# Mamba's half of an output projection moved in front of RWKV's inversion, for both segments at once

## The chip, the cores and the metric

One core of a Trainium2 chip runs the whole program in one launch. The metric is the device time in microseconds (us), the median of several executions.

## The reference

Two layers of a hybrid model over 256 context tokens (segment 0) and 256 latent tokens (segment 1), D = 1024, all in 32-bit floats. Each layer gets six modulation vectors per segment from `silu(c) @ w_ada + b_ada`. Layer 0 has an RWKV-7 mixer (8 heads of 64) and a Mamba-2 mixer (8 heads of 64) side by side; their outputs are concatenated, 512 columns each, and one projection `mix_w_out` (1024 x 1024) brings them back to the stream. A dense SwiGLU (2816 wide) follows. Layer 1 is a windowed attention in which only latent tokens ask, and a mixture of 8 experts. What the change is about:

```python
def finish(h, p, y_rw, y_mb):
    ...
    return jnp.concatenate([o_rw, y_mb], axis=-1).astype(h.dtype) @ w_out
...
h_lat = h_lat + m_lat[2] * o_lat
h_lat = h_lat + m_lat[5] * channel_mixer(_modulate(_rms_norm(h_lat, norm_ffn[i]), m_lat[3], m_lat[4]))
```

The same two lines stand for `h_ctx`. The projection is linear, so it can be made as RWKV's 512 rows of `w_out` plus Mamba's 512 rows.

## The kernel before

Activations lie with features on the 128 partitions and tokens along the free side: `hS[seg]` and `moS[seg]` are [128, 8, 256], block k holding features 128k to 128k+127. In `moS[seg]` blocks 0 to 3 are RWKV's output and 4 to 7 Mamba's.

**Weights.** Every weight is an entry of the list `stream`, in the order in which it is used: a chunk of 128 x 1024 floats, 512 KB (1 MB for the experts). `get_raw` (L82) hands out a chunk and emits loads up to 15 entries ahead, into a ring of four buffers `wraw`, all on SP's queue. So a chunk is loaded when the chunk four places earlier has been used up. `split_ws` (L374) turns a chunk into two halves of 128 x 512, and each into a rounded part `whi` (ScalarE, L393) and a rest `wlo` (L395, VectorE; GpSimd for every third chunk among the first 30 from `mo_first`). `project` (L399) makes three matmuls of 256 columns for each 128 x 128 block of weights and segment: hi x hi, lo weight x hi, hi weight x lo (L418).

**Modulation.** `ada_steps` (L281) multiplies the two vectors by 16 chunks of `w_ada`, eight matmul records a chunk (L290), and after each eighth chunk puts the sums in place by way of ScalarE (L295, L302) and GpSimd (L303). The first 16 chunks are made at the start. The other 80 steps, one chunk each, are a generator `ada_z`, and `tick(seg, n)` (L818) draws n steps of it while segment 0 is in the mixer, each tied behind the last PE instruction (`issue_after`). That is a lower bound only: a planner with a timeline of its own orders every engine's instructions when the program is built, so a step can stand later than its tick.

**The mixer of segment 0.** `mixer(0)` (L1113) handles both halves of RWKV's heads at once. `prepare` for each of four head pairs (11 ticks each) builds scaled operands, `operands` (2 ticks each) transposes them; then 8 ticks, then `invert` (L935): 31 steps of two VectorE instructions (L949, L951), each needing the one before, on tiles of 128 partitions. `merge` and the four steps of `chain` for each half (2 ticks in the first three) need the inverted blocks; then `finish` (L1075) in five rounds, one tick each, writes `moS`. All ticks that are left are drained, the context rows are loaded and transposed into `hS[0]` by `load_h` (16 transposes L1176, 4 copies L1177).

**After it.** `mixer(1)` (two halves one after the other, each with its own inversion) and `mix_ffn(0)` (L1208) are independent, and the planner interleaves them. `mix_ffn` projects `moS` in four column blocks of two chunks each (8 blocks of k), adds the gated result to `hS` (L1205), takes the norm's sums (squares on ScalarE, 16 matmuls with a column of ones, L352, for segment 0) and runs the SwiGLU. Then `load_h(1)` fetches x by GpSimd's queue into a tile of the next pool, and `mix_ffn(1)` follows. In layer 1's norm GpSimd adds up the four squares (L349).

## Time and profile before

| what | us |
|---|---|
| three timed runs | 1999.26, 2011.8, 2014.42 |
| median | 2011.8 |
| the profiled execution | 1999.02 |
| its span | 1997.1 |

The profile is of one execution, the one of 1999.02 us. Its stages, from the span's start: 0 to 230 the first modulation, input projection and Mamba; 237 to 302 RWKV's operands for segment 0; 302 to 340 the inversion; 340 to 385 merge and chain; 385 to 403 finish; 403 to 735 the SwiGLU of segment 0 among the mixer of segment 1; 757 to 778 the output projection of segment 1; then its SwiGLU, layer 1 and from about 1200 us on the experts. "x" is a count of records; PEclk is the share of the full TensorE clock that was granted (0.50 is 1.2 GHz, 1.00 is 2.4 GHz).

### The profile page before, as it was taken

What the parts mean: (1) busy time and instruction counts of PE and PEld (TensorE: products, weight loads), DVE (VectorE), ACT (ScalarE), POOL (GpSimd) and SP (SyncE); (2) the same over time, 40 slices, a digit from 0 to 9 for tenths busy, and PEclk for the clock granted to TensorE, in tenths of its full rate; (3) what the DMA queues carried; (4) which work ended last, traced back from release to release, by engine and by line L of the source; (5) the groups of instructions that cost most, each with busy time, mean ns of one, the idle gap of its engine ahead of it and who ended that gap; (6) DMA issues with size and microseconds to landing.
All of it is one profiled execution on the core that took longest, in us unless ns stands there. A gap on an engine that the chain in (4) does not pass through costs nothing.

```text
span 1997.1 us, 35257 instructions
## 1 busy us (share of the span) xinstructions
PE 1906.8 (95%) x13590; PEld 1610.6 (81%) x13590; DVE 1589.5 (80%) x2519; ACT 1225.1 (61%) x1912; POOL 204.1 (10%) x236
## 2 busy tenths in 40 slices
PE   6999997988999989999999979999999999999997
PEld 3886663777989989999999777888888888888885
DVE  5877677489599667666689768898999999999997
ACT  4555432345454455555578738777778787777775
POOL 4033230041120010000011220000000000000000
PEclk8999896988999999999999989999999999999998
DMA  7342388542335464555654548999999999999991
GB/s 277 104 111 85 115 284 292 175 142 87 118 101 175 128 177 145 170 182 181 199 165 131 201 158 319 355 347 347 354 362 362 332 363 354 361 334 356 347 351 53
DMA packets 266705, 459.34 MB, mean 230 GB/s; under 512 B 13325, under 2 KB 145585, under 8 KB 266529
## 3 DMA queue, kind: packets, MB, share of 16 engines
q1 hardware_dynamic: 257616, 438.80, 64.8%
q0 software_dynamic: 4496, 13.79, 2.3%
q10 hardware_dynamic: 4416, 4.41, 0.8%
q8 instruction: 109, 1.79, 0.4%
q14 instruction: 68, 0.55, 0.1%
HBM read 455.88 MB, written 1.08 MB: 229 GB/s over the span
## 4 chain that ended last, share of the span: by engine, by line
PE 85%; DVE 6%; DMA 5%; issue 2%; ACT 1%; POOL 1%; ACTq 0%; DVEq 0%; POOLq 0%
PE a L418 26%; PE b L1669 8%; PE b L1670 8%; PE b L1668 8%; PE ch L1719 4%; PE ch L1720 4%; PE ch L1718 4%; PE b L813 3%; DMA wraw<-in_w_ada_dram 3%; PE ch L813 2%; PE a L290 2%; PE y L418 2%; PE b L418 2%; DVE wlo L395 1%; PE y L813 1%
## 5 line engine op out<-in xcount | busy, mean ns | idle before, releaser
L395 DVE TENSOR_TENSOR wlo<-wraw,whi 128x1024 fp32r<-128x1024 f32 (+2 forms) x974 | 929.7, 975 | 203.2 <-ACT whi L393 193.7
L393 ACT ACTIVATE whi<-wraw 128x1024 fp32r<-128x1024 f32 (+2 forms) x996 | 830.9, 844 | 399.6 <-PE a L418 192.2
L1669 PE MATMUL b<-wlo,eH 128*128 128x512 f32 (+1 forms) x768 | 288.9, 376 | 2.0 <-DVE wlo L395 1.6
L1670 PE MATMUL b<-whi,eL 128*128 128x512 f32 (+1 forms) x768 | 285.5, 372 | 0.0
L418 PE MATMUL a<-xH,whi 128*128 128x256 f32 x928 | 267.8, 289 | 7.0 <-DVE su L1232 5.9
L1668 PE MATMUL b<-whi,eH 128*128 128x512 f32 (+1 forms) x768 | 272.7, 374 | 0.0
L418 PE MATMUL a<-xL,whi 128*128 128x256 f32 x928 | 267.3, 288 | 1.8 <-DVE xL L365 1.8
L418 PE MATMUL a<-xH,wlo 128*128 128x256 f32 x928 | 267.1, 289 | 0.9 <-DVE wlo L395 0.9
L418 PEld LDWEIGHTS a<-xH,whi 128*128 128x128 f32 x928 | 180.7, 195 | 10.7 <-DVE su L1232 6.2
L418 PEld LDWEIGHTS a<-xL,whi 128*128 128x128 f32 x928 | 180.5, 195 | 5.2 <-DVE xL L365 2.5
L418 PEld LDWEIGHTS a<-xH,wlo 128*128 128x128 f32 x928 | 180.0, 194 | 4.1 <-issue 1.6
L1669 PEld LDWEIGHTS b<-wlo,eH 128*128 128x128 f32 x768 | 144.8, 189 | 29.4 <-DVE wlo L395 5.0
L1668 PEld LDWEIGHTS b<-whi,eH 128*128 128x128 f32 x768 | 144.3, 188 | 26.7 <-ACT whi L393 1.5
L1670 PEld LDWEIGHTS b<-whi,eL 128*128 128x128 f32 x768 | 144.7, 188 | 24.8
L1719 PE MATMUL ch<-wlo,gH 128*128 128x512 f32 x352 | 140.2, 398 | 0.3 <-DVE wlo L395 0.3
L1720 PE MATMUL ch<-whi,gL 128*128 128x512 f32 x352 | 138.9, 395 | 0.0
L1718 PE MATMUL ch<-whi,gH 128*128 128x512 f32 x352 | 115.7, 395 | 0.0
L418 PE MATMUL a<-gL,whi 128*128 128x256 f32 x352 | 99.1, 284 | 1.0 <-DVE gL L372 1.0
L418 PE MATMUL a<-gH,whi 128*128 128x256 f32 x352 | 99.5, 286 | 0.0
L418 PE MATMUL a<-gH,wlo 128*128 128x256 f32 x352 | 98.8, 285 | 0.0
L290 PE MATMUL a<-wraw,cpad 128*32 128x256 f32 x768 | 71.5, 465 | 17.7 <-DMA wraw<-in_w_ada_dram 16.4
L1719 PEld LDWEIGHTS ch<-wlo,gH 128*128 128x128 f32 x352 | 66.1, 188 | 16.2 <-DVE wlo L395 1.0
(614 smaller groups left out, 3381.9 us busy)
## 6 DMA issues: line engine op xcount, KB each, us to landing
wraw<-in_moe_w_dram SPq DMA_DIRECT2D x254, 1024.0 KB, 6.2
wraw<-in_w_ada_dram SPq DMA_DIRECT2D x96, 512.0 KB, 5.3
wraw<-in_ffn_w_dram SPq DMA_DIRECT2D x88, 512.0 KB, 4.0
wraw<-in_na_w_qkv_dram SPq DMA_DIRECT2D x40, 512.0 KB, 3.7
wraw<-in_ffn_w_dram SPq DMA_DIRECT2D x48, 384.0 KB, 3.1
wraw<-in_mix_w_in_dram SPq DMA_DIRECT2D x24, 512.0 KB, 3.7
wraw<-in_mix_w_out_dram SPq DMA_DIRECT2D x16, 512.0 KB, 5.1
wraw<-in_moe_w_dram POOLq DMA_DIRECT2D x7, 1024.0 KB, 11.4
```

Of the source, the lines that this page charges most:

```text
L290: T.matmul(p[32 * j:32 * j + 32, 0:256], cpad[:, ko, :], w[:, 256 * j:256 * j + 256], start=ko == 0, stop=ko == KO - 1, skip_group_check=True)
L393: S.activation(hi, x, AF.Copy)
L395: (G if on_pool else eng or V).tensor_tensor(lo, x, hi.bitcast(F32), OP.subtract)
L418: T.matmul(bs[bi][0:m1 - m0, o:o + n], w_[:, k, m0:m1], x[part][:, kx, x[2]], start=bi not in begun, stop=last, skip_group_check=True)
L813: pe[0] = T.matmul(*args, **kw)
L1668: T.matmul(ps[k][:, 0:w], eH[:, ko, :], wh[:, i, :], start=ko == 0, stop=False)
L1669: T.matmul(ps[k][:, 0:w], eH[:, ko, :], wl[:, i, :], start=False, stop=False)
L1670: T.matmul(ps[k][:, 0:w], eL[:, ko, :], wh[:, i, :], start=False, stop=ko == KO - 1)
L1718: T.matmul(ps[n], gH[:, kf, :], wh[:, w, c_], start=kf == 0, stop=False)
L1719: T.matmul(ps[n], gH[:, kf, :], wl[:, w, c_], start=False, stop=False)
L1720: T.matmul(ps[n], gL[:, kf, :], wh[:, w, c_], start=False, stop=kf == 21)
```

## The change

- Mamba's output goes into a tile `moM` [128, 4, 512] for both segments, RWKV's into `moR`. `mamba_out` multiplies `moM` by Mamba's 512 rows of `mix_w_out`: it splits `moM` on ScalarE and GpSimd, then for each of four chunks (`split_ws(ci, G)`: rests on GpSimd) makes 24 matmuls of 512 columns, and ScalarE puts the sums, scaled by the gate, into a DRAM tensor `mom` by way of SP's queue, 256 KB at a time. It is called in three parts: after the operands of the third and fourth head pair, and in front of `invert`.
- `load_h` reads `mom` back (1 MB a segment), and VectorE adds the transposed rows to it. Segment 0's is called after the first round of `finish`; there the first chunk of RWKV's half is split too. Segment 1's stands in `mix_ffn(0)` behind the projection; x comes by the ring.
- The projections in `mix_ffn` have one chunk per column block in place of two.
- Modulation: 6 steps ahead of `mixer(0)`; 8 ticks in `prepare`, 2 in `operands` of the first two pairs, none in front of `invert`; 3, 3, 3, 1 in the chain's steps; 3 in each round of `finish`. In the stream Mamba's four chunks stand behind step 42, the context and RWKV's first chunk behind step 62.
- The norm's squares are taken column block by column block in `mix_ffn`; the first three are added on GpSimd, so 8 matmuls with ones are left.
- `zg` moves to another pool, so that segment 0's RWKV operands can be given up earlier.

```diff
@@ get_raw's stream
+    def between(n):
+        if n == 42:
+            for c0 in range(0, D, 256):
+                mom_ch.append(chunk(w_cols(a["mix_w_out"], 512 * D, D, range(4), c0, 256), (4, 256)))
+        if n == 62:
+            x_ch.extend(chunk(dram(a["ctx"], 128 * t * D, [[D, 128], [1, D]]), (D,)) for t in range(2))
+            mo_ch.append([mo_block(0)])
...
-        mo_ch.append([col_chunks(a["mix_w_out"], 0, D, c0, 256, KS) for c0 in range(0, D, 256)])
+        mo_ch[seg] += [mo_block(c0) for c0 in range(0 if seg else 256, D, 256)]
+        if seg == 0:
+            xl_ch = [chunk(dram(a["x"], 128 * t * D, [[D, 128], [1, D]]), (D,)) for t in range(2)]
...
+    def mamba_out():
+        moL = []
+        xh = []
+        for i in range(2):
+            xh.append(mt([128, 2, NT], "xmh", "BG", 2, F32R))
+            xl = []
+            for j in range(2):
+                S.activation(xh[i][:, j, :], moM[:, 2 * i + j, :], AF.Copy)
+                xl.append(wsp.tile([128, NT], F32R, name="moml", tag=("whi", "wlo")[j], bufs=nsplit[0]))
+                G.tensor_tensor(xl[j], moM[:, 2 * i + j, :], xh[i][:, j, :].bitcast(F32), OP.subtract)
+            moL += xl
+            if i == 0:
+                yield
+        xl = res.tile([128, 4, NT], F32R, name="moL", tag="h8")
+        for k in range(4):
+            S.activation(xl[:, k, :], moL[k].bitcast(F32), AF.Copy)
+        yield
+        for b, ci in enumerate(mom_ch):
+            ps = [bank("a b") for m in range(2)]
+            for ks, wh, wl in split_ws(ci, G):
+                for m in range(2):
+                    for k in range(ks.start, ks.stop):
+                        h, i = xh[k // 2][:, k % 2, :], k - ks.start
+                        w = slice(128 * m, 128 * m + 128)
+                        mm(ps[m], wh[:, i, w], h, start=k == 0, stop=False, skip_group_check=True)
+                        mm(ps[m], wl[:, i, w], h, start=False, stop=False, skip_group_check=True)
+                        mm(ps[m], wh[:, i, w], xl[:, k, :], start=False, stop=k == 3, skip_group_check=True)
+            for m in range(2):
+                ft = 2 * b + m
+                o = wsp.tile([128, NT], F32, name="momo", tag=("whi", "wlo")[m], bufs=nsplit[0])
+                for seg in range(2):
+                    t = slice(256 * seg, 256 * seg + 256)
+                    S.activation(o[:, t], ps[m][:, t], AF.Copy, scale=mods[0][:, 16 + ft, MOD[seg]:MOD[seg] + 1])
+                SY.dma_start(mom[128 * ft:128 * ft + 128, :], o)
...
+    def load_h(seg, chs, tag):
+        xt = [get_raw(i) for i in chs]
+        hS[seg] = (hcp, res)[seg].tile([128, KO, 256], F32, name="h", tag=("hc", "h8")[seg])
+        SY.dma_start(hS[seg], mom.rearrange("(k p) t -> p k t", p=128)[:, :, 256 * seg:256 * seg + 256])
+        for k in range(0, KO, 2):
...
+            V.tensor_tensor(h, p, h, OP.add)
...
@@ mixer
             if len(group) > 1:
-                tick(seg, 8)
+                next(m_)
                 X0s = unpack_both(AAs, invert(AAs))
...
+                if seg == 0 and hcp is None:
+                    context_next()
+                tick(seg, 3)
+    for _ in range(6):
+        next(ada_z)
     mixer(0)
@@ mix_ffn
-        for k in range(0, KO, 4):
-            split(x[0][:, k:k + 4, :], x[1][:, k:k + 4, :], moS[seg][:, k:k + 4, :], "s")
+        split(x[0][:, 0:4, :], x[1][:, 0:4, :], moS[seg], "s")
...
+            norm_sums(hS[seg], fp, 2 * i, acc, G)
+        if seg == 0:
+            load_h(1, xl_ch, "a")
```

## Rows read from the trace of the kernel before

**Rows 1.** The page's chain of waits that ended last, shares by engine.
```profile
PE 85%; DVE 6%; DMA 5%; issue 2%; ACT 1%; POOL 1%; ACTq 0%; DVEq 0%; POOLq 0%
```

**Rows 2.** Busy time by stage, core 0: stretch, its length, engines, PEclk, DMA share, GB/s.
```profile
237.20:302.10 64.90, 62.97 (x586) 38.73 (x582) 46.81 (x100) 19.33 (x50) 18.94 (x24) 0.93 0.86 282
302.10:340.00 37.90, 26.54 (x260) 9.90 (x256) 31.00 (x68) 9.13 (x20) 2.58 (x5) 0.70 0.92 309
340.00:385.30 45.30, 43.63 (x1056) 34.58 (x1048) 17.65 (x44) 14.01 (x38) 0.85 (x4) 0.83 0.57 188
385.30:402.50 17.20, 16.86 (x115) 8.07 (x113) 9.40 (x20) 7.37 (x12) 1.74 (x3) 0.90 0.56 167
402.50:412.70 10.20, 6.65 (x39) 5.18 (x39) 7.33 (x11) 6.75 (x15) 3.97 (x4) 0.69 0.60 201
412.70:455.00 42.30, 39.58 (x324) 35.17 (x324) 37.71 (x79) 19.14 (x38) 17.67 (x16) 0.95 0.40 121
455.00:500.00 45.00, 37.01 (x311) 33.59 (x310) 42.45 (x94) 23.54 (x44) 8.14 (x6) 0.85 0.28 83
500.00:735.00 235.00, 231.08 (x2484) 215.39 (x2484) 173.36 (x362) 114.69 (x218) 22.10 (x21) 0.99 0.44 133
735.00:757.00 22.00, 16.83 (x104) 15.74 (x102) 8.95 (x19) 8.25 (x14) 4.23 (x4) 0.77 0.78 180
757.00:778.00 21.00, 21.00 (x175) 20.76 (x174) 20.14 (x44) 13.61 (x25) 3.59 (x5) 1.00 0.48 151
```

**Rows 3.** Waits that ended in 235 to 345: us in total, times, longest.
```profile
PEld a L290 <- DMA wraw<-in_w_ada_dram: 25.2, 20, 3.4
PE a L290 <- DMA wraw<-in_w_ada_dram: 12.0, 16, 3.0
```

**Rows 4.** Line L290 (modulation) by stage: PE and PEld busy, records; eight are a chunk.
```profile
237.20:302.10 64.90, 24.11 (x292) 6.79 (x288) 0.93 0.86 282
302.10:340.00 37.90, 19.78 (x180) 4.19 (x176) 0.70 0.92 309
340.00:385.30 45.30, 9.04 (x112) 2.88 (x104) 0.83 0.57 188
385.30:403.40 18.10, 5.97 (x64) 1.85 (x64) 0.91 0.58 178
```

**Rows 5.** VectorE's groups in 302.1 to 340: busy, mean ns, idle time before.
```profile
L951 DVE TENSOR_TENSOR Xu<-Xu,tm 128x31 f32<-128x31 f32 (+15 forms) x31 | 10.6, 343 | 1.0
L949 DVE TENSOR_TENSOR tm<-Au,Xu 128x31 f32<-128x31 f32 (+15 forms) x31 | 10.6, 343 | 1.1
L313 DVE SCALAR_TENSOR_TENSOR g<-mod,PV 128x16 f32<-128x16 f32 x1 | 0.2, 176 | 4.7 <-POOL mod L303 4.7
```

**Rows 6.** Timeline of segment 1's first inversion beside GpSimd: start, us, engine, instruction.
```profile
457.23 0.38 DVE L951 TENSOR_TENSOR Xu<-Xu,tm 64x220 f32<-64x220 f32 x1
457.23 1.54 POOL L395 TENSOR_TENSOR wlo<-wraw,whi 128x512 fp32r<-128x512 f32 x1 [5.01 <-ACT whi L393]
457.64 1.38 DVE L949 TENSOR_TENSOR tm<-Au,Xu 64x231 f32<-64x231 f32 x1
```

**Rows 7.** The chain that ended last, in order of time: start, us, engine, line, records.
```profile
51.55 1.36 PE y L418 x6
...
458.75 4.50 PE a L352 x32
...
595.93 48.09 PE a L418 x399
```

**Rows 8.** GpSimd's rests of weights in 225 to 420: duration ns min/median/max, first and last start.
```profile
L395 POOL TENSOR_TENSOR wlo<-wraw,whi x2: 1266/1336/1405, 406.7 to 408.0; 128x512 fp32r<-128x512 f32 x2
```

**Rows 9.** VectorE in 385 to 413, an addition of 128 x 512.
```profile
L1106 DVE TENSOR_TENSOR yrw<-yrw,moc 128x512 f32<-128x512 f32 x2 | 1.4, 692 | 0.1
```

**Rows 10.** Waits that ended in 730 to 805.
```profile
ACT sq L348 <- issue: 4.5, 1, 4.5
PE a L1176 <- DVE h L1205: 4.0, 1, 4.0
```

More of the change, by code (lines that the diff above doesn't have):

```diff
@@ L39, in hybrid_kernel @@
     cscr = dp.tile([16, NT], F32, name="cscr")
+    mom = dp.tile([D, NT], F32, name="mom")
     def dram_row(t, n):
@@ L158, in hybrid_kernel @@
     hS = [None, None]
-    moS = [res.tile([128, KO, 256], F32, name="moc", tag="h8"), res.tile([128, KO, 256], F32, name="mol")]
+    moM = res.tile([128, 4, NT], F32, name="moM", tag="h8")
+    moR = res.tile([128, 2, 4, 256], F32, name="moR", tag="mol")
+    moS = [moR[:, seg] for seg in range(2)]
     c0 = pool(c0s, "c0")
@@ L393, in split_ws @@
                 S.activation(hi, x, AF.Copy)
-            on_pool = 0 <= i - mo_first and (lambda n, k: n<30 and n%3==0)(i - mo_first, k0 // step)
+            on_pool = 0 <= i - mo_first and i < mo_first + 30 and (i - mo_first) % 3 == 0
             (G if on_pool else eng or V).tensor_tensor(lo, x, hi.bitcast(F32), OP.subtract)
@@ L397, in split_ws @@
         return out_
+    ready = {}
     def project(chs, xs, use, w=256, tag="a"):
@@ L410, in project @@
         for k0, ci in chs:
-            for ks, wh, wl in split_ws(ci):
+            for ks, wh, wl in ready.pop(ci, None) or split_ws(ci):
                 for i, (m0, m1) in enumerate(ms):
@@ L559, in hybrid_kernel @@
     S.dma_start(gup, a["rw_g_up"][0])
+    zg = [mkp.tile([96, 256], F32, name=f"zg{seg}") for seg in range(2)]
     mbs = ctx.enter_context(ExitStack())
@@ L706, in hybrid_kernel @@
             for seg in range(2):
-                y = moS[seg][:, 4 + hp, :]
+                y = moM[:, hp, 256 * seg:256 * seg + 256]
                 tk = slice(256 * seg, 256 * seg + 256)
@@ L715, in hybrid_kernel @@
             sq = bt([128, NT], "sqm", "cb", bufs=2)
-            for seg in range(2):
-                S.activation(sq[:, 256 * seg:256 * seg + 256], moS[seg][:, 4 + 2 * g_ + h, :], AF.Square)
+            S.activation(sq, moM[:, 2 * g_ + h, :], AF.Square)
             for j in range(4):
@@ L726, in hybrid_kernel @@
             for seg in range(2):
-                y = moS[seg][:, 4 + hp, :]
+                y = moM[:, hp, 256 * seg:256 * seg + 256]
                 V.scalar_tensor_tensor(y, y, pv("mnw", hp), p[:, 256 * seg:256 * seg + 256], OP.mult, OP.mult)
@@ L1295, in values_of @@
         return last
-    load_h(1, [xt[:, t] for t in range(2)])
     for r2 in range(2):
```

99 lines of the change are left out of this document (58 added, 41 removed).

## The prediction

> **What bounds the kernel now.** I read the chain of waits first: PE holds 85% of it [rows 1], so work taken off PE counts where PE has no gaps. Busy time by stage says where that is [rows 2]: in 500 to 735 PE is busy 231.08 of 235 us, in 757 to 778 all 21.00, both at full clock. Other stages end otherwise. In 237 to 302 PE is busy 62.97 of 64.9 us, but 24.11 us of that are modulation matmuls, 36.5 chunks [rows 4]. In 302 to 340 the DMA rings run at 309 GB/s, PE waits for modulation chunks (25.2 and 12.0 us from 235 to 345 [rows 3]) and nobody minds, because VectorE's inversion ends this stage; that chain is held 4.7 us by one instruction that waits for a modulation sum [rows 5]. In 340 to 403 merge, chain and finish step between PE, ScalarE and VectorE, with the DMA rings half idle (0.57 and 0.56). In 402.5 to 412.7 PE is busy 6.65 us at a clock of 0.69: finish is over, the context's transposes and the first weights are not there. From 412.7 to 500 VectorE is busy 37.71 of 42.3 and 42.45 of 45 us, PE 39.58 and 37.01. In 735 to 757 PE has 16.83 of 22 us at a clock of 0.77 [rows 2].
>
> The idea of the change follows from this: PE is idle or on work nobody waits for while VectorE inverts, and the projection can lie there. I go through it stage by stage against the profiled execution, 1999.0 us (span 1997.1 and 1.9 around it).
>
> **Operands, 237 to 302.** Six modulation chunks are used up before the mixer, and each head pair draws 8 ticks in place of 11. A chunk costs PE 24.11/36.5 = 0.66 us here [rows 4]. Six of them are 4 us, but they now stand in Mamba's stage, where PE is busy too; I take half, and 3 us for waits on chunks that come later: -5 us. Ends: 0, if the planner puts the same number of steps before the inversion as now (36 of the 42 still fit), and -10, if all six and all waits go.
>
> **The inversion, 302 to 340.** The 4.7 us go: by the count of records (36.5 chunks up to 302 and 22.5 in the inversion [rows 4]) the sum that L313 waits for, half-way in, comes of chunk 48 of 80, and after the change only 42 are drawn by then. Against it stands GpSimd. Twelve of its instructions of 128 x 512 are new here (four rests of `moM`, eight of weights), 1.27 to 1.41 us each [rows 8], and none runs during the inversion today. What one does to an inversion is to be seen at 457: the step beside it takes 1.38 us, its neighbour of nearly the same size 0.38 [rows 6], so 1.0 us is lost; at least ten of the twelve fall into the inversion: +10 us. Together +5; ends: -5 (all twelve before it) and +12 (12 x 1.0, and the stall only moved).
> The Trainium skill, SBUF — State Buffer, section Who interferes with whom, states that a VectorE instruction with two SBUF inputs and a GpSimd instruction that reads SBUF exclude one another for a whole instruction. The two rows agree in kind; by the rule up to 1.34 us could be lost each time, 13 us in place of 10, and the time below would be 1981.
>
> Does PE finish under it? Mamba's half is 4 chunks x 24 = 96 matmuls of 512 columns. Six take 1.36 us [rows 7], 0.227 each: 21.8 us, twice that at 1.2 GHz. PE's own work in this stage is 26.54 - 19.78 = 6.8 us [rows 2, 4], so they are ready some 10 to 14 us into the inversion, whose VectorE part is then 38 - 4.7 + 10 = 43 us long: end after 36, or 58 at the low level throughout. I take 0, ends 0 and +15. The put to DRAM (8 x 256 KB) finds the rings free, since no modulation is drawn until the chain: 0, at most +5 for the 4 MB written and read back at about 309 GB/s with part of them exposed; the reading of `mom` stands 40 us behind the put. No row shows a store of this kind, hence the bound.
>
> **Merge, chain, finish, 340 to 403.** Here the steps come back: 20 ticks in the chain for 12, 15 in finish for 5, 18 more on a path where PE is one of the links. A chunk costs 9.04/14 = 0.65 us [rows 4], 11.7 us in all; where PE waits for a copy it is hidden. I take half, +6; ends 0 and +12. The rings: 4 of Mamba's chunks, 38 of modulation, the context's 2 and RWKV's first come behind step 42. A chunk of 0.524 MB at 309 GB/s takes 1.70 us; the chain needs 16 new ones in 45 us and is not starved.
>
> **From finish to the first projection, 402.5 to 412.7.** The context's transposes and the first weights stand ready now, and half of `moS` is to be split. But behind the chain the ring still has 17 chunks of modulation and 3 of RWKV's half to load, 20 x 1.70 = 34 us, against 27.4 from the chain's end to the first matmul today. So only the first block starts early: -3; ends -9 and +5. The additions on VectorE, 0.69 each [rows 9], replace copies on ScalarE.
>
> **The projection of segment 0, 412.7 to 500.** 96 of 192 matmuls of 256 columns go, 48.09/399 = 0.1205 us each: 11.6 us. Half of the 32 records with ones go: 2.25 of 4.50 us [rows 7]. PE is within 3 us of full up to 455 and short in the gap after it, where an earlier SwiGLU fills what the inversion leaves. Sum -14; ends: -5, if VectorE is the bound there (it loses splits of weights, but gains four additions of 0.69 us), and -16.
>
> **735 to 778.** Segment 1's 16 transposes leave the transition; PE waits 4.0 us with them behind VectorE, and ScalarE stands 4.5 us behind an issue [rows 10]: the first goes, the second needn't. -5 of the 22 us; ends 0 and -9. Then another 96 matmuls, here with no gap at all: 96 x 0.1205 = -11.6; ends -9 and -12. Layer 1's norms trade one addition on GpSimd for four matmuls: 0, +-2.
>
> **Sum.** -5 + 5 + 6 - 3 - 14 - 5 - 11.6 = -27.6, so 1971.4 for an execution like the profiled one. That one equals the fastest of the three timed runs; their median, 2011.8, is 12.8 us higher. Nothing in the profile says which of the two a new median will be like, so I add half of it: 1978.
>
> **The rivals.**
> *The gaps fill up* (for it: the 8 us without PE in 455 to 500 and the 10 us of 402.5 to 412.7; against it: VectorE is 94% busy there). The 18 ticks are hidden (-6), the start gains its full 9 (-6), and the SwiGLU runs under the inversion (-12): 1978 - 24 = 1954.
> *The first projection isn't shortened*: it is late by its weights (34 us of loads behind the chain) and by VectorE, not by PE. For it: VectorE's 37.71 of 42.3 us and a ring of four. Then the -14 goes and the -3 becomes +5: 1978 + 22 = 2000, no change that can be told.
> *Mamba's half doesn't lie under the inversion but ahead of merge* (the slower side). Its rests and weight splits go through GpSimd, which VectorE holds up in turn; if the matmuls get going only when the inversion ends, and at 1.2 GHz as PE does in this stage now (clock 0.70, then 0.83 [rows 2]), 96 x 0.454 = 43.6 us stand on the path: 1978 + 43.6 = 2021.6, slower than before. It decides from 27.6 us on, that is from about three fifths of the matmuls exposed at that level. Against it: PE comes into the inversion from a stage with a clock of 0.93, and the twelve GpSimd instructions are only 16 us.
>
> **How the numbers follow.** Forecast 0.50, gaps filled 0.20, no shorter projection 0.20, ahead of merge 0.10. The worst ends added up reach +43 us and the best -63, but not together. 8 in 10: from 1948, just below the first rival, to 2010, half-way into the last one. About 1% (20 us) is what a measurement can tell from no change: faster means under 1992. The forecast gives 0.45 of that (14 us of margin) and 0.05 same; the first rival 0.20 faster; the second 0.01 faster, 0.18 same, 0.01 slower; the last 0.05 same and 0.05 slower. Together 0.66, 0.28, 0.06.
>
> **What would show it.** Right: the inversion free of the 4.7 us idle time but with about ten steps of 1.3 us beside GpSimd; 96 matmuls of 512 columns that end before merge; modulation records up in 340 to 403 from 22 to about 38 chunks; both projections at 96 matmuls of 256 columns; the stretch of 21 us at 757 cut by more than 9. Wrong: merge's first matmul more than 45 us after the inversion's first transpose; PE waiting for chunks in the chain; a projection of segment 0 that ends no earlier after the chain than now; or an output projection of segment 1 that isn't shorter because its weights are late.

## The result, and the profile after

The changed kernel takes 2028.9 us (median of 20 runs, 2007.5 to 2039.4), the kernel before 2005.9 beside it (20 runs, 1994.3 to 2017.7): the ratio is 1.009, 95% interval 1.0066 to 1.0115. It is slower by 0.9% (the medians lie 23.0 us apart), where 1978 was forecast; that lies outside the range too. The time of an execution goes with its mean granted clock: the four shortest of the changed kernel, 2007.5 to 2018.3 us, have 0.962 to 0.966, the five longest, 2034.7 to 2039.4, have 0.952 to 0.954, and nine of ten executions of the kernel before (those timed beside the experiments) lie between 0.960 and 0.967. The profiled execution took 2034.9 us, 2033.1 from first to last instruction, against 1997.1 before: 36.0 us more, since it is one of the long ones and the one of the kernel before a short one.

I cut both executions at the same instructions. *Operands* runs from 237.2 to the inversion's first VectorE step, *inversion* from there to the start of its last full transpose (tile `XT`), *merge and chain* to ScalarE's copy of the first Y, *finish* to the first matmul of segment 0's projection, *projection and SwiGLU 0* to the last matmul of its down projection, *to SwiGLU 1* to the first down-projection matmul of segment 1; the rest is layer 1.

| stage, us | before | after | difference |
|---|---|---|---|
| operands | 68.8 | 91.1 | +22.3 |
| inversion | 30.1 | 35.1 | +5.0 |
| merge and chain | 47.6 | 63.5 | +15.9 |
| finish | 29.0 | 52.2 | +23.2 |
| projection and SwiGLU 0 | 326.5 | 309.5 | -17.0 |
| to SwiGLU 1 | 98.0 | 84.6 | -13.4 |
| rest | 1159.9 | 1159.9 | 0 |

So the gain is there, 30.4 us, and in front of it 66.4 us are lost. The chain of waits that ended last, by engine, hardly shows it: PE has 86% where it had 85% [rows 1].

```profile
PE 86%; DVE 8%; DMA 4%; ACT 1%; issue 1%; POOL 0%; ACTq 0%; SPq 0%; DVEq 0%
```

The stages show it. Busy time of the changed kernel by stage, columns as in [rows 2]: stretch, length, PE, PEld, DVE, ACT, POOL, PEclk, DMA share, GB/s.

```profile
237.20:323.90 86.70, 84.36 (x556) 52.25 (x555) 47.85 (x102) 19.48 (x49) 20.01 (x26) 0.68 0.64 198
323.90:367.00 43.10, 30.32 (x218) 21.01 (x216) 40.80 (x68) 20.34 (x42) 15.10 (x13) 0.85 0.41 137
367.00:428.00 61.00, 56.07 (x1089) 41.46 (x1090) 17.86 (x44) 17.73 (x47) 4.93 (x7) 0.85 0.68 230
428.00:479.00 51.00, 45.61 (x273) 22.99 (x272) 24.25 (x49) 12.00 (x25) 10.84 (x14) 0.67 0.69 220
479.00:536.00 57.00, 46.08 (x351) 40.37 (x350) 51.28 (x113) 28.95 (x56) 15.39 (x15) 0.94 0.32 96
536.00:789.00 253.00, 246.75 (x2664) 230.60 (x2664) 195.74 (x408) 119.73 (x232) 26.63 (x21) 0.98 0.42 129
789.00:797.00 8.00, 4.45 (x20) 4.16 (x20) 4.22 (x7) 3.61 (x6) 2.96 (x4) 0.63 1.03 212
797.00:812.00 15.00, 15.00 (x106) 14.47 (x107) 10.69 (x23) 7.90 (x16) 1.80 (x2) 0.86 0.63 145
```

The first row answers to 237 to 302 in [rows 2]: PE has fewer instructions (556 for 586) and is busy 84.36 us for 62.97, at a granted clock of 0.68 for 0.93. DMA has room there (0.64). The second row has the rings at 0.41 where they ran at 0.92. The fourth, between chain and projection, is 51 us long where the kernel before has 27.4, with the clock at 0.67.

The modulation line, L317 now, by the same stages (PE and PEld busy with records, PEclk, DMA share, GB/s; eight records are a chunk), answers to [rows 4]:

```profile
237.20:323.90 86.70, 27.11 (x264) 6.79 (x264) 0.68 0.64 198
323.90:367.00 43.10, 1.71 (x24) 0.58 (x24) 0.85 0.41 137
367.00:428.00 61.00, 12.81 (x160) 3.40 (x160) 0.85 0.68 230
428.00:479.00 51.00, 16.58 (x144) 4.08 (x144) 0.67 0.69 220
```

33 chunks cost PE 27.11 us before 323.9 (0.82 each, 0.66 forecast), three stand just behind, ahead of the inversion's first step, 20 in merge and chain, 18 behind it. That count is as forecast; the 18 at 0.92 us each are not.

VectorE in the inversion, its two groups of steps (busy, mean ns, idle time before), answers to [rows 5]: 31.1 us for 21.2. No instruction there waits for a modulation sum any more.

```profile
L1025 DVE TENSOR_TENSOR Xu<-Xu,tm 128x31 f32<-128x31 f32 (+15 forms) x31 | 15.6, 502 | 1.1
L1023 DVE TENSOR_TENSOR tm<-Au,Xu 128x31 f32<-128x31 f32 (+15 forms) x31 | 15.5, 499 | 1.0
```

The timeline beside it (start, us, engine, line, instruction) shows why, as [rows 6] did: the steps beside a GpSimd rest take 1.38 and 1.40 us, the next one of nearly the same size 0.43.

```profile
344.06 2.83 POOL L428 TENSOR_TENSOR wlo<-wraw,whi 128x512 fp32r<-128x512 f32 x2 [6.34 <-PE b L847]
344.36 1.38 DVE L1023 TENSOR_TENSOR tm<-Au,Xu 128x255 f32<-128x255 f32 x1
345.77 1.40 DVE L1025 TENSOR_TENSOR Xu<-Xu,tm 128x255 f32<-128x255 f32 x1
347.20 0.43 DVE L1023 TENSOR_TENSOR tm<-Au,Xu 128x256 f32<-128x256 f32 x1
```

Mamba's 96 matmuls begin at 334.4 and end at 380.9, 15.5 us behind the last full transpose's end. Three of the four blocks (a block is one chunk's 24 matmuls) are done at 358.0, ahead of that transpose. The fourth's rests stand in GpSimd's queue behind the copies of `AA`, which wait for the transpose (timeline of GpSimd):

```profile
365.36 2.12 POOL L1055 COPY AA<-XT 32x1024 f32<-32x1024 f32 x2 [11.41 <-DVE XT L1047]
367.56 2.48 POOL L428 TENSOR_TENSOR wlo<-wraw,whi 128x512 fp32r<-128x512 f32 x2
```

So the chain that ended last (start, us, what) has the fourth block in the middle of merge, where 22 of its 24 matmuls of 512 columns take 2.43 + 2.13 + 0.43 + 0.43 + 1.36 + 1.18 = 8.0 us:

```profile
372.38 2.43 PE a L847 x5
374.81 2.13 PE b L847 x5
376.94 0.43 PE a L847
377.37 0.43 PE b L847
377.80 0.52 PE ch L847 x8
378.32 1.36 PE a L847 x5
379.67 1.18 PE b L847 x5
```

And SP's own queue (timeline, same columns) shows what holds the loads of chunks: a put of `mom` waits 10.85 us in it for an eviction, which stands in ScalarE's queue behind the inversion's copies; the next chunks are issued at 370.06 and 383.74:

```profile
357.79 10.85 SPq L894 DMA_DIRECT2D mom<-momo  x2
370.06 0.33 SPq L78 DMA_DIRECT2D wraw<-in_w_ada_dram  x1
380.64 1.43 SPq L894 DMA_DIRECT2D mom<-momo  x2
383.74 0.33 SPq L78 DMA_DIRECT2D wraw<-in_w_ada_dram  x1
```

The chain that ended last then goes through the load of a chunk, in the middle of the chain of RWKV's steps:

```profile
384.76 8.74 DMA wraw<-in_w_ada_dram
393.54 0.64 PE a L317 x8
```

### The profile page after: what moved, and what is told of

It reads as the page before. It is cut to its first block, busy times and chain, and to the rows that moved or that the text cites. A ratio compares the mean times of both kernels' runs of the same rounds, so it can differ in the third digit from the quotient of the medians.

```text
span 2033.1 us, 35072 instructions
## 1 busy us (share of the span) xinstructions
PE 1934.0 (95%) x13502; PEld 1623.9 (80%) x13502; DVE 1591.1 (78%) x2509; ACT 1220.0 (60%) x1912; POOL 218.9 (11%) x245
## 4 chain that ended last, share of the span: by engine, by line
PE 86%; DVE 8%; DMA 4%; ACT 1%; issue 1%; POOL 0%; ACTq 0%; SPq 0%; DVEq 0%
PE a L453 26%; PE b L1760 8%; PE b L1761 8%; PE b L1759 8%; PE ch L1810 4%; PE ch L1811 4%; PE ch L1809 4%; PE b L847 4%; PE ch L847 2%; DMA wraw<-in_w_ada_dram 2%; PE y L453 2%; PE a L317 2%; PE b L453 2%; DVE wlo L428 1%; PE y L847 1%; PE b L1384 1%
## 5 line engine op out<-in xcount | busy, mean ns | idle before, releaser
L428 DVE TENSOR_TENSOR wlo<-wraw,whi 128x1024 fp32r<-128x1024 f32 (+3 forms) x958 | 912.9, 975 | 190.4 <-ACT whi L426 183.1
L453 PE MATMUL a<-xH,whi 128*128 128x256 f32 x864 | 248.8, 289 | 7.6 <-ACT xH L404 3.1
L453 PE MATMUL a<-xH,wlo 128*128 128x256 f32 x864 | 248.0, 288 | 4.4 <-DVE wlo L428 4.4
L453 PE MATMUL a<-xL,whi 128*128 128x256 f32 x864 | 248.8, 288 | 1.4 <-DVE xL L398 1.4
L453 PEld LDWEIGHTS a<-xH,whi 128*128 128x128 f32 x864 | 168.0, 195 | 10.7 <-ACT xH L404 3.3
L453 PEld LDWEIGHTS a<-xH,wlo 128*128 128x128 f32 x864 | 167.6, 194 | 7.5 <-DVE wlo L428 5.1
L453 PEld LDWEIGHTS a<-xL,whi 128*128 128x128 f32 x864 | 167.7, 194 | 3.5 <-DVE xL L398 1.8
L1809 PE MATMUL ch<-whi,gH 128*128 128x512 f32 x352 | 115.7, 395 | 0.0
L317 PE MATMUL a<-wraw,cpad 128*32 128x256 f32 x768 | 73.3, 481 | 17.8 <-DMA wraw<-in_w_ada_dram 16.5
L1810 PEld LDWEIGHTS ch<-wlo,gH 128*128 128x128 f32 x352 | 66.1, 188 | 16.2 <-DVE wlo L428 1.0
## 6 DMA issues: line engine op xcount, KB each, us to landing
wraw<-in_moe_w_dram POOLq DMA_DIRECT2D x7, 1024.0 KB, 12.7
```

Of the source, the lines that this page charges most:

```text
L317: T.matmul(p[32 * j:32 * j + 32, 0:256], cpad[:, ko, :], w[:, 256 * j:256 * j + 256], start=ko == 0, stop=ko == KO - 1, skip_group_check=True)
L428: (G if on_pool else eng or V).tensor_tensor(lo, x, hi.bitcast(F32), OP.subtract)
L453: T.matmul(bs[bi][0:m1 - m0, o:o + n], w_[:, k, m0:m1], x[part][:, kx, x[2]], start=bi not in begun, stop=last, skip_group_check=True)
L1809: T.matmul(ps[n], gH[:, kf, :], wh[:, w, c_], start=kf == 0, stop=False)
L1810: T.matmul(ps[n], gH[:, kf, :], wl[:, w, c_], start=False, stop=False)
```

## Experiments

Eighteen kernels ran, each beside the kernel before. Times are medians, ratios are to the kernel before with their 95% intervals, stages are of the one profiled execution of each.

### The clock of the operands

**changed_again**: the changed kernel, no edit.


> The changed kernel once more, for a second profile. Theory A1 (the clock of the operands stage goes with how the modulation matmuls are placed, so the half clock belongs to this kernel): 237 to the inversion's first step at 84 us or more again with a granted clock under 0.8. Rival (it is a matter of the single execution): 75 us or less, as in the kernels with the front as before.


2032.5 us, ratio 1.0134 (1.0099 to 1.0168). Operands 85.0 us at a clock of 0.79 (0.62 in 240 to 270, 0.83 in 270 to 300): just inside theory A1's figures, far from the rival's.

**front_as_before**: front of the kernel before, Mamba's half and the late edits kept.
```
-        if n == 42:          # chunk positions of Mamba's weights and of ctx
+        if n == 52:
-        if n == 62:
+        if n == 72:
-        tick(seg)            # two places in prepare
+        tick(seg, 2)
-            if hp < 2:
-                tick(seg)
+            tick(seg)        # operands
-    for _ in range(6):
-        next(ada_z)
```


> Only the front put back (no 6 in front of the mixer, 11 + 2 per head pair: 52 chunks drawn before the inversion); the inversion has none, the chain keeps its 20. Theory A1 (the operands' half clock comes of fewer modulation matmuls between the head pairs' own): 237 to the first inversion transpose falls from 87 to 65 to 70 us with PE's granted clock at 0.9 or more, though 16 more chunks are multiplied there; the whole 2000 to 2015. Rival (the half clock has another cause, so that each of the 16 chunks costs 1.0 us more): the stage lasts 95 us or more and the whole stays at 2025 or above.


2008.7 us, ratio 1.0008 (0.9988 to 1.0028): as fast as the kernel before, 20 us under the changed one. Operands 72.7 us, clock 0.90 (240 to 270) and 0.94 (270 to 300). 52 chunks are drawn ahead of the inversion for 42, but the planner lays many of them into it: the stage itself has 296 modulation records (37 chunks) for the changed kernel's 288, and the kernel before has 300. PE's records in all are 610, 606 and 612. So the fronts differ in the clock and in where the matmuls stand, not in how many there are; that part of A1 isn't borne out.

**more_matmuls**: ten chunks' matmuls of that stage twice.
```
+                    if 22 <= drawn[0] < 58 and drawn[0] % 3 == 2 and ko < KO - 1:
+                        T.matmul(p[...], zeros, w[...], start=False, stop=False, ...)
```


> The changed kernel with the matmuls of ten of the 36 modulation chunks of the operands stage issued twice, the second time with weights of zero (the sums stay the same); nothing else moves. Theory A1 (the clock falls because PE has too little work between the head pairs' own matmuls): the granted clock in 237 to 324 rises from 0.68 to over 0.85 and the stage gets shorter than 87 us in spite of ten chunks' more work. Rival (the clock there has nothing to do with how much modulation work there is): clock as before at 0.68, the stage 6 to 10 us longer, the whole 5 to 10 us above the changed kernel.


2035.6 us, ratio 1.0144 (1.0098 to 1.019). Busy time and clock in the two halves of the stage, the changed kernel first, then this one (columns as above):

```profile
240.00:270.00 30.00, 29.02 (x156) 16.54 (x155) 17.56 (x43) 6.07 (x16) 10.27 (x13) 0.56 0.65 187
270.00:300.00 30.00, 30.00 (x164) 19.75 (x168) 13.98 (x29) 5.67 (x14) 4.90 (x8) 0.56 0.47 148
```

```profile
240.00:270.00 30.00, 29.01 (x224) 17.43 (x223) 19.33 (x47) 6.61 (x18) 12.98 (x16) 0.76 0.66 202
270.00:300.00 30.00, 30.00 (x271) 19.84 (x272) 19.08 (x39) 11.32 (x28) 4.62 (x7) 0.89 0.72 248
```

With more to do the stage takes 81.5 us for 91.1 and 85.0: PE does more records in the same 30 us at the higher clock. Over the stage the clock is 0.85 where the changed kernel has 0.68 and 0.79. That fits A1, if less than it asked; it is one profile. The whole got no shorter: the first projection starts 8.5 to 17.8 us earlier, and projection and SwiGLU 0 take 321.7 us for 309.5 and 316.0.

**six_early**: the front as before, with the six chunks ahead of the mixer as in the changed kernel.


> The kernel with the front as before, but with the six chunks in front of the mixer as the changed kernel has them (58 drawn before the inversion). It tells apart which of the two edits of the front brings the half clock. Theory A1 (too few ticks per head pair): operands stage as in the front as before or shorter, first inversion step at 304 to 318, granted clock 0.85 or more in 260 to 300. Rival (six early chunks start PE and the rings earlier and the clock falls for it): first step at 322 or later, clock 0.5 to 0.7 in 240 to 290.


2013.8 us, ratio 1.005 (1.0015 to 1.0084). First step at 316.5, operands 79.3 us, clock 0.53 at 240 and 1.00 from 270: inside A1's band (0.92 in 260 to 300). In this profile the six chunks alone don't bring the long stage.

What the other runs add weakens the word "belongs". *half_between_ticks* and *second_read_later* (below) have, but for records missing from the traces, the same order of PE instructions up to the inversion. The first:

```profile
240.00:270.00 30.00, 29.89 (x242) 17.60 (x240) 22.11 (x50) 8.35 (x21) 11.66 (x13) 0.91 0.85 281
270.00:300.00 30.00, 28.63 (x301) 18.23 (x300) 21.70 (x44) 10.87 (x28) 6.26 (x8) 1.00 0.85 294
```

The second:

```profile
240.00:270.00 30.00, 27.70 (x154) 16.79 (x150) 17.74 (x41) 6.16 (x16) 8.20 (x9) 0.61 0.69 225
270.00:300.00 30.00, 30.00 (x205) 18.16 (x207) 15.89 (x29) 8.25 (x20) 6.01 (x8) 0.70 0.58 181
```

Operands take 68.7 us in one and 86.8 in the other, and their spans differ by 18.6: one order of PE instructions, two clocks. *front_as_before*, *plan_as_before* and *splits_ahead* share another order up to there and take 72.7, 80.8 and 81.1. The changed front was profiled five times and took 91.1, 85.0, 91.1, 89.5 and 86.1 us; the fuller fronts, the kernel before's among them, 67 to 81 us in thirteen profiles and 86.8 in one.

### The late chunks

**sixteen_left_out**: the changed kernel without the last 16 chunks.
```
-    for l, q in ((0, 1), (0, 2), (1, 0), (1, 1), (1, 2)):
+    for l, q in ((0, 1), (0, 2), (1, 0), (1, 1)):
```


> The changed kernel with the last 16 of its 80 modulation chunks left out, loads and matmuls (the last third of layer 1's modulation is a constant). They all stand behind the chain. It prices a late chunk. Theory H (each late chunk stands on the path from the copy of Y to the first projection with its load, 1.2 to 1.7 us): that stretch falls from 52 to 25 to 32 us, the whole 15 to 25 us under the changed kernel. My forecast (0.33 us for each): 5 to 7 us.


2010.2 us, ratio 1.0034 (1.0008 to 1.006). Finish takes 21.7 us for 52.2 and 47.9, even below H's 25 to 32: 26 to 31 us for 16 chunks, 1.6 to 1.9 each. The whole is 19 to 22 us under the changed kernel. Theory H, not my 0.33.

**before_sixteen_left_out**: the same cut in the kernel before.


> The kernel before with its last 16 modulation chunks left out, loads and matmuls, as in sixteen left out: the control to that price. There they are drawn in the chain and in finish, beside other work. Theory H (a late chunk costs its load only because the changed kernel has 38 of them behind the inversion, more than the rings bring in time): here the first projection starts only 5 to 12 us earlier (0.3 to 0.7 us for each chunk), against 30 us for the same 16 chunks in the changed kernel. Rival (each chunk on this stretch costs its 1.7 us wherever it stands): 22 us or more.


2002.4 us, ratio 1.0002 (0.9968 to 1.0036): nothing at all. Not even H's 5 us came. The kernel before, in merge and chain and behind finish:

```profile
340.00:370.00 30.00, 28.55 (x701) 21.89 (x694) 10.67 (x27) 9.23 (x26) 0.42 (x2) 0.75 0.62 209
400.00:415.00 15.00, 11.45 (x77) 8.47 (x76) 10.94 (x22) 9.47 (x19) 3.97 (x4) 0.77 0.57 176
```

Without the 16 chunks:

```profile
340.00:370.00 30.00, 29.30 (x532) 21.60 (x532) 9.06 (x20) 8.97 (x23) 1.42 (x3) 0.50 0.47 156
400.00:415.00 15.00, 13.63 (x35) 7.06 (x33) 9.31 (x16) 5.52 (x9) 0.00 (x0) 0.50 0.29 89
```

PE's records fall from 701 to 532 and the clock from 0.75 to 0.50: over merge and chain the clock is 0.64 for 0.80. In this profile what the chunks had cost came back as a lower clock; that their going lowered it is one reading, not a test.

**inversion_eight**: eight ticks behind Mamba's half, twelve in the chain.
```
                next(m_)
+                tick(seg, 8)
...
-        tick(seg, 3 if c < 3 else 1)
+        if c < 3:
+            tick(seg, 2)
```


> The changed kernel with 8 ticks behind Mamba's half in the inversion and 12 in the chain in place of 20; the front stays as changed. Theory A2 (the DMA rings stand idle in the inversion because no chunk is drawn there, and the late chunks keep the chain waiting): the waits for chunks in 370 to 482 fall from 17.7 us to under 10, merge to first projection is 10 to 20 us shorter, operands stay at 87; the whole 2008 to 2020. Rival (SP's queue is held by the puts of mom in that time, so chunks can't be loaded earlier whatever is drawn): the first projection starts within 5 us of 479, the whole within 5 us of the changed kernel.


2027.8 us, ratio 1.0117 (1.0088 to 1.0146). From the last transpose to the first projection 103.0 us for 115.7 and 112.5, so 9.5 to 12.7 shorter, at the edge of theory A2's band; the whole stays with the changed kernel, as the rival had it (its first projection, at 461.3, is 8.5 to 17.8 us earlier, as the rival had not). Projection and SwiGLU 0 gives 7 us of it back against the first profile (316.9 for 309.5).

**plan_as_before**: all ticks of the kernel before, Mamba's half kept (front_as_before and inversion_eight together).


> The changed kernel with the modulation ticks put back where the kernel before has them: none in front of the mixer, 11 + 2 per head pair (52 chunks before the inversion), 8 behind Mamba's half in the inversion, 12 in the chain. Mamba's half by DRAM, the early loads and the early x stay. Theory A (the loss of the front, 66 us, comes of where the modulation chunks are drawn: operands at half clock, and 38 chunks left for merge, chain and finish): operands again in 65 to 70 us, merge, chain and finish at most 10 us longer than before, the first projection's first matmul at 425 to 440 us, the whole 1970 to 1990. Rival B (Mamba's half itself costs it: the put and the reading of mom hold SP's queue, GpSimd's rests hold VectorE, the fourth block stands ahead of merge): merge to finish stays 20 us or more longer than before, the whole 2000 or more.


2014.1 us, ratio 1.0042 (1.0016 to 1.0069). Finish is 27.3 us, shorter than before's 29.0, but merge and chain 69.1 for 47.6. Operands take 80.8 us, not A's 65 to 70, though the ticks are those of the kernel before. Theory A falls as the whole cause: with no chunk drawn later than before, 21.5 us of merge and chain stay (15.5 in front_as_before). What is left there is Mamba's half with its loads and its put.

### Mamba's half

**half_left_out**: its weights' splits and its matmuls out of the changed kernel (the four rests of `moM` stay).
```
-            for ks, wh, wl in split_ws(ci, G):
-                ...
+            w = get_raw(ci)
+            for m in range(2):
+                mm(ps[m], w[:, 0, 128 * m:128 * m + 128], xl[:, 0, :].bitcast(F32), start=True, stop=True)
```


> The changed kernel with the splits and the 96 matmuls of Mamba's half left out (one plain matmul a bank stands for them; loads, evictions, puts and readings stay, h isn't the reference's). It prices the half where it stands. Theory G (the half lies on the path behind the inversion, by its blocks' splits and by its place in PE's queue): from the inversion's last transpose to the copy of Y 48 to 53 us in place of 63.5, the inversion's own 35 us 4 us shorter, the whole 12 to 20 us under the changed kernel. My forecast (the half hidden under the inversion): from last transpose to the copy of Y within 4 us of 63.5, the whole at most 6 us shorter.


2018.7 us, ratio 1.0053 (1.0023 to 1.0083): 10 to 14 us under the changed kernel. Inversion 29.4 for 35.1, merge and chain 55.3 for 63.5. The stages are G's but for 2 us in merge, and the whole is at or under the lower end of its band. The 8.2 us in merge and chain match the fourth block's 8.0; VectorE's two groups fall by 5.8 us:

```profile
L1020 DVE TENSOR_TENSOR Xu<-Xu,tm 128x31 f32<-128x31 f32 (+15 forms) x31 | 12.7, 410 | 1.1
L1018 DVE TENSOR_TENSOR tm<-Au,Xu 128x31 f32<-128x31 f32 (+15 forms) x31 | 12.6, 408 | 1.0
```

**Why more of it stands on the path in the fuller front** is read from GpSimd's timeline in front_as_before. The first block's rests start at 333.81, though the inversion began at 309.9 (ScalarE's split ahead of them waited 5.6 us for the load of the block's weights); the copies of `AA`, which wait for the inversion's end, stand between the second block's two rests; and a block follows the other every 7 to 10 us:

```profile
333.81 2.61 POOL L428 TENSOR_TENSOR wlo<-wraw,whi 128x512 fp32r<-128x512 f32 x2 [6.01 <-ACT whi L426]
342.21 1.29 POOL L428 TENSOR_TENSOR wlo<-wraw,whi 128x512 fp32r<-128x512 f32 x1 [5.79 <-ACT whi L426]
343.99 2.13 POOL L1054 COPY AA<-XT 32x1024 f32<-32x1024 f32 x2 [0.49 <-DVE XT L1046]
346.20 1.27 POOL L428 TENSOR_TENSOR wlo<-wraw,whi 128x512 fp32r<-128x512 f32 x1
351.93 2.53 POOL L428 TENSOR_TENSOR wlo<-wraw,whi 128x512 fp32r<-128x512 f32 x2 [4.46 <-ACT whi L426]
```

The matmuls lie from 333.8 to 365.5, three quarters of it behind the last transpose's start at 341.9. Four kernels tried to mend that.

**splits_ahead** (on front_as_before): the next block's split ahead of the evictions.
```
-            for ks, wh, wl in split_ws(ci, G):
+            for ks, wh, wl in ws:
...
+            if b < 3:
+                ws = split_ws(mom_ch[b + 1], G)
```


> The kernel with the front as before, with one more edit: the weights of Mamba's next block are split ahead of the evictions of the block in hand. Theory C (Mamba's four blocks run one after the other, each waiting for split, rest, matmuls and eviction in turn, some 8 us a block for 5.5 us of matmuls, so the third and fourth stand on PE ahead of merge): the four blocks take 22 to 26 us in place of 33, the stretch from the inversion's last transpose to the copy of Y falls from 63 to 53 to 57 us, the whole 1998 to 2004. Rival (blocks wait for something else, GpSimd's queue or SP's): blocks still 30 us or more, the whole within 3 us of 2009.


2017.2 us, ratio 1.0058 (1.004 to 1.0077). The blocks take 32.0 us (341.7 to 373.7) for 31.7: theory C falls. The whole is 8.5 us over front_as_before, which the rival hadn't either; the profile had the slower operands (81.1).

**rests_on_vector** (on front_as_before): `split_ws(ci)` for `split_ws(ci, G)`.


> The kernel with the front as before; the rests of Mamba's weights are computed on VectorE in place of GpSimd. Theory D (GpSimd is what stretches the blocks: 1.3 us a rest, and the third block's wait behind the copies of AA that wait for the inversion): the blocks take 26 us or less, inversion's first step to last transpose within 2 us of 32 (eight rests of 0.7 us come, the GpSimd stalls go), the whole 3 to 10 us shorter than 2009. Rival (VectorE is the bound in the inversion and its queue is in order, so rests there wait for inversion steps or hold them up): inversion 35 us or more and the whole the same or longer.


2019.6 us, ratio 1.0069 (1.0042 to 1.0096). Inversion 31.5 for 32.0, but blocks 35.4 us, merge and chain 73.8 for 63.1. Theory D has the inversion right and the rest wrong. Finish is 11.5 us shorter, so the first projection starts no later (440.7 for 442.0); the profile's loss lies behind it, in projection and SwiGLU 0 (327.0 for 316.1).

**puts_left_out** (on front_as_before): no put; `h` reads weights in place of `mom`.


> The kernel with the front as before, with the puts of Mamba's half to DRAM left out; in place of mom the same number of bytes of the weights is read, so h isn't the reference's. Theory B (puts hold SP's queue and keep modulation chunks from being loaded, and a block waits for the put of an earlier one to give its buffer back): chain and finish wait less for chunks, first projection at 430 or before in place of 442, the whole 8 us or more shorter. Rival (a put lands in 2 us and nothing waits for it; the loads stand still because the ring's four slots are full): first projection within 3 us, the whole within 3 us of 2009.


2019.6 us, ratio 1.009 (1.0055 to 1.0124): longer than with the puts. The first projection starts at 443.7 for 442.0, as the rival had it, so in that front nothing was gained by freeing SP. But the edit moved more than it took away: the planner that orders the instructions put merge's and Mamba's matmuls in another order on PE, and merge and chain took 74.4 us for 63.1. So the run doesn't price the puts. Where its time goes isn't shown either: the profiled execution, 2012.07, is one of its shortest.

**half_between_ticks**: 48 chunks in front, splits ahead, two ticks behind each block, two in every step of the chain.
```
+        for c0 in {48: (0, 256), 50: (512,), 52: (768,)}.get(n, ()):
...
+            tick(0, 2)       # mamba_out, behind each block's matmuls
...
-        tick(seg, 3 if c < 3 else 1)
+        tick(seg, 2)
```


> A version that follows from the theories on the clock, the ring and the blocks: 48 chunks in front (11 per head pair, 2 more for the first two pairs, none in front of the mixer), Mamba's blocks split one ahead, with two modulation ticks behind each block's matmuls, 16 in the chain. Where theory E holds (the ring of four stands still while Mamba's blocks hold it and no chunk is drawn, so the loads come late), the first projection starts at 425 to 432 in place of 442, and the whole is 1990 to 2000, faster than both kernels. Rival (DMA from the inversion to the first projection is not the bound): as splits ahead alone, within 3 us.


2010.0 us, ratio 1.0036 (1.0015 to 1.0057). Merge and chain 57.9 us, finish 35.8, first projection at 433.7: the earliest of all versions with the half, but 2 us short of E's band there, and the whole is 10 us short of it, still slower than the kernel before and no faster than front_as_before (2008.7).

**between_ticks_no_half**: the same without the half's splits and matmuls.


> Half between ticks with the splits and the 96 matmuls of Mamba's half left out (one plain matmul a bank stands for them; h isn't the reference's). It prices the half where its chunks are not late. Theory G (the half is on the path there too, by its place on PE ahead of merge): the first projection 8 to 15 us earlier, the whole 6 to 14 us under half between ticks. Rival (with ticks between its blocks the half lies under the inversion and the loads): at most 4 us earlier.


1993.4 us, ratio 0.9949 (0.9924 to 0.9975). The half costs 16.6 us even there, a little over G's band. The profiled execution had the slower operands (78.1), so its first projection starts only 2.4 us earlier; from the inversion's first step to there it is 116.0 us for 127.8. With the half at no cost, this version would gain 12 us on the kernel before.

### The late edits

**late_parts_alone**: the kernel before with segment 1's x loaded by the weight stream and transposed behind segment 0's projection, and the norms' sums by GpSimd.
```
+            norm_sums(hS[seg], fp, 2 * i, acc, G)
+        if seg == 0:
+            load_h(1, xl_ch)
```


> The kernel before with two late edits of the change alone: x of segment 1 comes by the weight stream and is transposed behind segment 0's projection, and the norms' squares are summed by GpSimd block by block. No half of Mamba in the inversion, the modulation chunks where they were. Theory F (these parts are worth what the changed kernel shows between the end of segment 0's SwiGLU and segment 1's projection, 14.3 to 3.5 us there, and some 2 us a norm): the whole 7 to 12 us under the kernel before. Rival (VectorE is the bound up to 520, and the 16 transposes and copies only move in front of it): within 3 us of the kernel before.


2010.1 us, ratio 1.0032 (1.0015 to 1.0048): slower, by 7 us. Projection and SwiGLU 0 takes 334.0 us for 326.5, and to SwiGLU 1 98.4 for 98.0. The chain that ended last says why nothing comes back. In the kernel before (and PE's wait behind the load, from the timeline):

```profile
734.63 13.29 DMA misc<-in_moe_router_w_dram
748.05 3.55 PE L1383 MATMUL y<-misc,mod 128*128 128x8 f32 x16 [0.33 <-DMA misc<-in_moe_router_w_dram]
```

and in this one:

```profile
740.90 13.93 DMA misc<-in_moe_router_w_dram
```

It is the load of the router's weights, whose matmuls stand in PE's queue between the norm's and the projection's. PE is idle for it only 0.33 us in the kernel before (1.68 here), since the first transposes and the norm's sums end just ahead of it. So the 4.0 us that PE waited with the transposes couldn't come back: the load's end stood 0.33 us behind that work. I read the transposes as the price because they were the longest waits of PE shown [rows 10].

**norm_sums_alone**: the kernel before with the sums only.


> The kernel before with the norms' sums of squares by GpSimd, block by block, alone; x stays late. My forecast for this part was 2 us less for segment 0. Theory I (early x is what costs): within 3 us of the kernel before, or 2 us shorter. Rival (GpSimd's additions hold VectorE up where it is the bound, as in the inversion): 4 us or more longer than the kernel before, as with both late edits.


2008.0 us, ratio 1.0016 (0.9985 to 1.0047): no difference that can be told.

**x_late**: half_between_ticks with x of segment 1, and its part of `mom`, where the kernel before has x.


> Half between ticks, with segment 1's x loaded and transposed, and its part of mom read, where the kernel before has x: behind segment 0's SwiGLU. Theory I (early x is no gain: the stretch behind the SwiGLU is held by the 14 us load of the router's weights in either case, while the 16 transposes and additions in front of it cost 5 to 8 us): the stretch from segment 0's first projection to its last SwiGLU matmul 4 to 8 us shorter than with x early, nothing lost behind it, the whole 4 to 8 us under half between ticks (2002 to 2006). Rival (early x is worth what I gave it, 5 us): the whole 4 us or more over half between ticks.


2021.1 us, ratio 1.0073 (1.0041 to 1.0106): theory I falls for half_between_ticks, which takes 11 us less. Projection and SwiGLU 0 is 11 us shorter (309.3 for 320.3), but to SwiGLU 1 takes 105.9 for 88.5, so by these two stages early x is worth 6.4 us; in the operands this profile had 78.8 us for 68.7. (The reading of `mom` is late there as well; the two weren't told apart.) Early x was no gain beside the kernel before and is one here.

**second_read_later**: half_between_ticks with segment 1's reading of `mom` held behind segment 0's projection.


> Half between ticks, with segment 1's reading of mom (1 MB) held behind segment 0's projection; x stays early. Theory J (both readings stand among the last modulation chunks on rings that then carry 300 GB/s, so the second takes 3 to 4 us from them): the first projection starts 3 to 4 us earlier, the whole 2 to 5 us shorter. Rival (the rings have room, or the transposes of x now wait for the reading): within 2 us, or longer.


2015.9 us, ratio 1.0049 (1.0019 to 1.008). Finish 35.4 us for 35.8: theory J falls. The profile has the half clock shown above.

## Why the prediction was wrong

**Operands: -5 forecast, +22.3 (second profile +16.2).** The step that failed is that the rest of PE's work in the stage was left at its old price; the sum has the chunks and their waits and nothing for the clock. In the changed kernel 292 records that aren't modulation took 84.36 - 27.11 = 57.25 us, where 294 had taken 62.97 - 24.11 = 38.86 [rows 2, 4]: 18.4 of the 21.4 us that PE has more. The chunks cost 0.82 each in place of the 0.66 read in a stage at 0.93. The front put back takes some 20 us off the whole. The cause of the lower clock stays open. The number of PE's records up to the inversion's first step, 606 after and 612 before, doesn't tell the two fronts apart; the changed front had the long stage in all five profiles, the clock was higher in the one run with doubled chunks, and one order of PE instructions was seen at either clock. The Trainium skill, TensorE: Matmul & The Clock Gate, Part 1, says that the clock of the array is gated by how busy the array itself was. The trace doesn't contradict it, with 271 records in 30 us at 0.89 where 164 ran at 0.56, but a higher clock also lets more records through; and with 30.00 busy us of 30.00 at 0.56, the profile's busy PE can't be read for it.

**Inversion: +5 forecast, +5.0.** Right by its steps: the wait for the modulation sum is gone, ten of the twelve GpSimd instructions stand in it, and VectorE's 62 steps take 9.9 us more beside them, where +10 was set. The six rests of weights make 5.8 of these, by half_left_out.

**Mamba's half: 0 forecast, 8.0 us behind the inversion; 10 to 17 us of the whole by the runs without it.** The inputs were ready as forecast: the matmuls began 10.5 us behind the inversion's first transpose (323.9), from which the prediction counts. "End after 36" is the step that failed; they ended after 57. That is near the 58 given for a low clock throughout, but came by waits, at a clock of 0.85. PE's time was summed (21.8 us), not the queues that feed it: each block goes through ScalarE, GpSimd, PE and ScalarE again, and the fourth's rests stand in GpSimd's queue behind copies that wait for the inversion's end. "PE comes into the inversion from a stage with a clock of 0.93" failed with the operands. What came is the third rival in part: the fourth block ahead of merge with 8.0 us, the first half of it at a low clock (2.43 us for five matmuls, 1.36 later), below the 27.6 us from which that rival decides. It was not enough alone.

**Late chunks: +6 forecast for chain and finish, -3 behind them; merge and chain +15.9, finish +23.2.** Two steps failed. "The chain needs 16 new ones in 45 us and is not starved" counted the rings' rate; the ring of four held Mamba's chunks while SP stood 10.85 us behind a put, the rings ran at 0.41, and the chunks then came late: one load of 8.74 us stands on the chain of waits. That "where PE waits for a copy it is hidden. I take half" took the price from the kernel before, where the control shows it to be zero; here it is 1.6 to 1.9 us each. That the put "finds the rings free", at 0, was right of the rings and missed the queue; what that alone costs stayed open.

**Projection 0 and SwiGLU: -14 forecast, -17.0. To SwiGLU 1: -16.6 forecast, -13.4.** The sum is right, in part by luck. The -17.0 is -10.5 in the second profile, and the versions with the half have 306.8 to 327.0 us in that stage, so it can't be put to the 96 matmuls alone. The -13.4 falls into three: 14.3 us before the projection runs on became 8.3 (-6.0 for -5), the projection's 24.4 became 14.8 (-9.6 for -11.6, within the ends), and what follows grew by 2.2. The -6.0 didn't come as argued: the transposes' wait was worth 0.33 us, and the router's 16 matmuls (3.55 us) now stand behind the projection's start. In their place GpSimd's sums stand in the chain:

```profile
790.68 1.28 POOL sq L371
792.02 1.28 POOL sq L371
793.35 3.58 PE ch L385 x16
```

The further back the edits lie, the better they were forecast; the front was priced by counts of work at the old clock, and that is where it went wrong. One sum of the prediction doesn't come out: its worst ends as listed add up to +37 us, not +43 (the best do make -63); no chance hangs on it.

**What stays open**: why the clock of the operands takes either level with one order of PE instructions, and why the changed front had the low one in each profile (its four shortest runs, at mean clocks of 0.962 to 0.966, weren't profiled); what part of the late chunks is SP's held queue and what the full ring; whether a placement of Mamba's half exists that costs less than 16 us in the fuller front. The three prices (front some 20 us, half 10 to 17, late chunks 19 to 22) can't be added: together they exceed the loss. No version that computes the whole beat the kernel before; front_as_before equals it.

## What to carry to other kernels

A price read at one TensorE clock holds at that clock: find the stage's clock, treat it as part of what is changed, and price the work that stays in the stage as well as the work that is moved. Work moved under another engine's chain must be followed through every queue that feeds it (ring slots, the engines that split and evict, what stands ahead in each), not summed on its own engine. And before a wait is priced at a transition, follow the chain that ended last through it: the longest wait listed needn't be the one that holds, and a path that ends 0.33 us behind another gives back no more than that.

## What was not expected of the hardware

The same order of PE instructions took 68.7 us in one execution and 86.8 in another, with granted clocks of 0.91 and 1.00 against 0.61 and 0.70, and the spans of the two versions differ by 18.6 us. Sixteen chunks of matmuls, left out of the kernel before, gave 0 us (ratio 1.0002), and the clock of their stage fell from 0.75 to 0.50.
